# Mixer of a Griffin/attention trunk: four units in the first loop, other places for the first recurrences and the last gates, an output projection in two sums, and modulation rows one per tick

## The chip, the cores and the metric

The kernel runs on one core of a Trainium2 chip. The metric is the device time of one execution in microseconds (us).

## The reference

Two layers on a stream of 1024 frames of width 1024, all in float32. Layer 0 (the mixer, where the change is) is:

```
hn = rms_norm(x) * (1 + scale) + shift          # shift, scale: rows of c_act @ ada_w
gate, xr = split(hn @ w_in)                     # 2 x 1408 columns, 11 tiles of 128 each
xr = causal_depthwise_conv(xr, width 4)
r, i = sigmoid(blocks(xr) @ w_a), sigmoid(blocks(xr) @ w_x)     # 16 blocks of 88 columns
a = exp(-8 * r * softplus(-lam));  u = sqrt(1 - a*a) * (i * xr)
y = scan(y = a * y + u)                         # along the frames
h = x + g1 * ((y * gelu(gate)) @ w_out)
h = h + g2 * (relu(modulated_norm(h) @ w1)**2 @ w2)             # the MLP
```

Layer 1 is chunked attention with an MLP of the same form.

## The kernel before

Every matmul is three (`mm3`, lines L324 to L326): operands are split into a high part (ScalarE, L191) and a low part (VectorE, L195 for weights and for y, L907 for the conv's result, L601 and L792 for normed activations). Activations lie transposed, 128 columns by 1024 frames, so one unit (`proj2`: one tile of 128 columns, both halves of 512 frames) is 48 matmuls.

A class `Stream` lists all that is loaded in order: weights (kind "w"), operands y (kind "a"), modulation rows (kind "u", summed on VectorE at L357) and pre-sums of quadrants (kind "p", L123). It loads through a ring of seven buffers on SyncE's queue, and in each `tick` of the program emits the splits, rows and pre-sums that are due, in list order and as far as a cap per kind lets them. `some(n)` and `gate_item` put rows and the blocks' gate weights into the list; `ws.at(d, ...)` puts work d ticks later. So the order on each engine is what the program writes, tick by tick, and each engine takes its own in that order.

The mixer begins with a loop over the eight tiles of the normed input, in which the norm's work is done tile by tile and the matmuls of the first three units (xr(0), xr(1), gate(0)) accumulate in PSUM at the same time. Then come single units: `xr(t)` makes a tile of xr (ScalarE L879 and L881 take it out of PSUM, VectorE L886 is the conv), copies issued by GpSimd (L894) re-lay the conv's result into blocks of 88 columns, which are split (L900 on ScalarE, L907 on VectorE); `recur(blocks)` does the blocks' gates (sigmoids L933, the product i*x L938, tanh L945, roots and exp L950 and L953) and the scan (L957 to L961); `gate(t)` does a tile of the gate with gelu (L873), and L974 multiplies it with the scan's result, which is stored and loaded again as y. At the end w_out is applied in three sums c = 0, 1, 2 over 3, 4 and 4 tiles of y, each with all eight chunks of 128 output columns; each chunk goes into h at L1059 (`into_h`). Next to the last of them begins the second norm (sq L520, mod L583, statistics L528 to L538), and then the MLP, whose first product w1 is formed by seven products of quadrants (L1209 and L1129 add them).

PSUM has eight banks of 512 columns; a new bank waits until the one that it replaces has been read.

Of the kernel before, what the change touches and what calls it, by code (L numbers as in the profile page):

```python
# [16 lines left out]
KD = 8  # L17
# [48 lines left out]
class Stream:  # L66
# [8 lines left out]
    def __init__(self, nc, slot, wh, ws):  # L75
# [8 lines left out]
        self.hold = None  # L84
        self.timed = self.early = False
# [74 lines left out]
    def ready(self, it, kind, most):  # L160
# [138 lines left out]
def trunk(ctx: ExitStack, tc: tile.TileContext, I, out, dbg=None, stop=None):  # L299
# [102 lines left out]
    w_in(NT, NT + 1, 0, NT + 2, 1)  # L402
    gate_item(_done(0) + _done(1))
    for t in range(3, NT):
        w_in(NT + t)
        some(2 if t < 7 else 0)
        gate_item(_done(t - 1))
        if t < NT - 1:
            w_in(t - 1)
    w_in(NT - 2)  # L410
    gate_item(_done(NT - 1))
    w_in(NT - 1)
    ygd = dp.tile([NT, 128, S], F32, name="ygd")
    ygits = []
    for c in range(3):
        kn = 4 if c else 3
        for _ in range(kn):
# [3 lines left out]
        for j in range(4):  # L421
            ws.add(I["w_out"][c * 4 + j][:, : kn * 256], kn * 256)
            some((2, 2, 0)[c])
# [78 lines left out]
    class Norm:  # L502
# [20 lines left out]
        def mm(self, half):  # L523

            ps = bank()
# [16 lines left out]
        def bc(self, half):  # L542
            ps = bank()
# [195 lines left out]
    for k in range(3, KD):  # L739
# [55 lines left out]
    n1.mm(0)  # L795
    ws.pump(2)
    n1.bc(0)
# [15 lines left out]
    def unit():  # L813
        first.append(ws.next())
        pss.append([bank(), bank()])

    def products(us, half, k):
        c = slice(k * 128, (k + 1) * 128)
        for u in us:
            it = first[u]  # L820
# [4 lines left out]
    unit()  # L825
    unit()
# [3 lines left out]
    n1.mm(1)  # L830
    products((0, 1), 0, 1)
    ada_k(2)
    n1.bc(1)
    moded(2, 0)
    lows(2, 0)
    unit()
# [7 lines left out]
    ada_k(3)  # L844
    for k in range(3):
        lows(k, 1)
        products((0, 1, 2), 1, k)
    for k in range(3, KD):
        moded(k, 0)
        lows(k, 0)  # L850
        normed(1, k)
        if k < KD - 1:
            ada_k(k + 1)
        moded(k, 1)
        lows(k, 1)
        products((0, 1, 2), 0, k)
        products((0, 1, 2), 1, k)
        if k == 6:
            ws.pump(4)
# [95 lines left out]
    def scan(b):  # L955
# [3 lines left out]
        V.tensor_scalar(out=r, in0=r, scalar1=-1.0, scalar2=1.0, op0=ALU.mult, op1=ALU.add)  # L959
        V.tensor_tensor(out=v, in0=v, in1=x, op=ALU.mult)  # L960
# [50 lines left out]
    for half in range(2):  # L1011
        xr_out(0, half, pss[0][half])
    for half in range(2):
        xr_out(1, half, pss[1][half])
    conved(0)
    gelu(0, pss[2])
    for it in first:
        at(1, ws.done, it)
    at(2, conved, 1)
    ws.pump()  # L1020
    xr(2)
    gate(1)
    recur(_done(0) + _done(1))
    for t in range(3, NT):
        xr(t)
        recur(_done(t - 1))
        if t < NT - 1:
            gate(t - 1)
    gate(NT - 2)
# [8 lines left out]
    ws.cap["a"] = 6  # L1038
    gate(NT - 1)
# [4 lines left out]
    k0 = 0  # L1044
    for c in range(3):
        kn = 4 if c else 3
        ys = ygits[k0 : k0 + kn]
        k0 += kn
        its = [ws.next() for _ in range(4)]
        ws.cap["a"] = (14, 16, 8)[c]  # L1050

        def chunk(j, half, e):

            m, it, ps = 2 * j + e, its[j], bank()
            for k in range(kn):
                s = slice(k * 256 + e * 128, k * 256 + e * 128 + 128)
                gh, gl = ys[k]["op"][half]
                mm3(ps, it["hi"][:, s], it["lo"][:, s], gh, gl, k == 0, k == kn - 1)
            V.scalar_tensor_tensor(out=h[m][:, hs(half)], in0=ps, scalar=g1[:, m : m + 1],  # L1059
                                   in1=h[m][:, hs(half)], op0=ALU.mult, op1=ALU.add)  # L1060
            if c == 2:
                final = (half, m) == (1, KD - 1)
                at(int(m < KD - 1), n2.sq, m, hs(half), int(m < KD - 2))

        if c < 2:
            for j in range(4):
                for half in range(2):
                    for e in range(2):
                        chunk(j, half, e)
                        if c == 0 and (j, half, e) in ((0, 0, 1), (0, 1, 1)):  # L1070
                            load_h(2)
                        tick()
                at(1, ws.done, its[j])
        else:

            for j in range(4):
                for e in range(2):
                    chunk(j, 0, e)
                    tick()
            for j in range(4):  # L1080
                for e in range(2):
                    chunk(j, 1, e)
                    n = 2 * j + e
                    if n == 1:
                        n2.mm(0)
                    elif n == 3:
                        n2.bc(0)
                    elif n > 3:
                        n2.mod(0, (n - 4,))
                    ws.tick()  # L1090
                ws.done(its[j])
        ws.live["a"] -= 2 * kn
# [669 lines left out]
```

## Time and profile before

| | |
|---|---|
| median of 3 runs | 2388.7 us (2388.6, 2395.36, 2388.7) |
| profiled execution | 2395.81 us, its span 2394.0 us |
| TensorE busy | 2287.7 us (96%) |
| VectorE busy | 1763.6 us (74%) |
| ScalarE busy | 1246.2 us (52%) |
| TensorE's mean granted clock | 0.985 |
| DMA, mean over the span | 152 GB/s |

A busy share is a mean over all stages; 1.00 of the clock is the full one of 2.4 GHz, 0.50 the lower of its two levels. The mixer's matmuls end at about 490 us of the span.

### The profile page before, as it was taken

What the parts mean: (1) busy time and instruction counts of PE and PEld (TensorE: products, weight loads), DVE (VectorE), ACT (ScalarE), POOL (GpSimd) and SP (SyncE); (2) the same over time, 40 slices, a digit from 0 to 9 for tenths busy, and PEclk for the clock granted to TensorE, in tenths of its full rate; (3) what the DMA queues carried; (4) which work ended last, traced back from release to release, by engine and by line L of the source; (5) the groups of instructions that cost most, each with busy time, mean ns of one, the idle gap of its engine ahead of it and who ended that gap; (6) DMA issues with size and microseconds to landing.
All of it is one profiled execution on the core that took longest, in us unless ns stands there. A gap on an engine that the chain in (4) does not pass through costs nothing.

```text
span 2394.0 us, 31739 instructions
## 1 busy us (share of the span) xinstructions
PE 2287.7 (96%) x11740; PEld 1935.6 (81%) x11740; DVE 1763.6 (74%) x2596; ACT 1246.2 (52%) x2052; POOL 398.7 (17%) x419
## 2 busy tenths in 40 slices
PE   4999989999999899999999999999999999899999
PEld 3778767878877777888999998998888888778887
DVE  8797779588777777778765648997386666778775
ACT  5677873265544643334443229997165555634342
POOL 0001000000000023331000038875000000033322
PEclk9999989999999999999999999999999999999999
DMA  8343349326666774546244200013214444865443
GB/s 306 101 133 106 104 120 314 109 69 220 245 227 236 267 268 147 161 146 228 88 145 131 96 10 10 10 37 122 95 45 165 169 158 163 285 238 161 155 149 133
DMA packets 141640, 363.46 MB, mean 152 GB/s; under 512 B 14924, under 2 KB 17100, under 8 KB 141484
## 3 DMA queue, kind: packets, MB, share of 16 engines
q1 hardware_dynamic: 113756, 278.45, 35.3%
q10 hardware_dynamic: 23824, 71.44, 7.8%
q0 software_dynamic: 3904, 11.54, 1.9%
q8 instruction: 92, 1.51, 0.3%
q14 instruction: 64, 0.52, 0.1%
HBM read 260.19 MB, written 89.65 MB: 146 GB/s over the span
## 4 chain that ended last, share of the span: by engine, by line
PE 65%; DVE 13%; DMA 9%; ACT 8%; issue 4%; POOL 1%; SPq 0%; ACTq 0%; DVEq 0%; POOLq 0%
PE b L325 20%; PE b L326 20%; PE b L324 20%; DMA ws<-in_w_dram 3%; DVE wl L195 2%; DMA hid<-s 2%; PE b L1568 1%; DVE s L195 1%; ACT s L1538 1%; DVE s L357 1%; DMA ws<-hid 1%; ACT s L329 1%; DVE s L1129 1%; POOL ws L123 1%; PE b L1587 1%
## 5 line engine op out<-in xcount | busy, mean ns | idle before, releaser
L324 PE MATMUL b<-s,wh 128*128 128x512 f32 (+1 forms) x2532 | 1004.2, 397 | 43.3 <-DVE s L1231 11.7
L325 PE MATMUL b<-s,wh 128*128 128x512 f32 (+1 forms) x2532 | 998.7, 394 | 19.4 <-DVE s L907 6.5
L326 PE MATMUL b<-s,wl 128*128 128x512 f32 (+1 forms) x2296 | 905.4, 394 | 4.1 <-DVE wl L195 4.1
L324 PEld LDWEIGHTS b<-s,wh 128*128 128x128 f32 (+1 forms) x2532 | 480.0, 190 | 165.0 <-DVE s L1209 13.9
L325 PEld LDWEIGHTS b<-s,wh 128*128 128x128 f32 (+1 forms) x2532 | 479.8, 189 | 128.1 <-DVE s L907 7.4
L191 ACT ACTIVATE wh<-ws 128x1024 fp32r<-128x1024 f32 (+2 forms) x302 | 291.1, 973 | 441.6 <-POOL ws L123 261.1
L326 PEld LDWEIGHTS b<-s,wl 128*128 128x128 f32 (+1 forms) x2296 | 435.1, 190 | 100.1 <-DVE wl L195 5.8
L195 DVE TENSOR_TENSOR wl<-ws,wh 128x1024 fp32r<-128x1024 f32 (+2 forms) x249 | 305.8, 1231 | 113.8 <-ACT wh L191 111.5
L1231 DVE SCALAR_TENSOR_TENSOR s<-b,mod,s 128x512 f32<-128x512 f32 x221 | 165.0, 747 | 88.3 <-PE b L326 88.0
L195 DVE TENSOR_TENSOR s<-ws,s 128x512 fp32r<-128x512 f32 x284 | 223.4, 805 | 0.3 <-ACT s L191 0.3
L123 POOL TENSOR_TENSOR ws<-ws 128x512 f32<-128x512 f32 x21 | 28.4, 1354 | 1165.2 <-DMA s<-hsp 922.3
L324 PE MATMUL b<-wh,s 128*128 128x256 f32 x768 | 216.4, 284 | 0.0
L325 PE MATMUL b<-wl,s 128*128 128x256 f32 x768 | 216.0, 283 | 0.0
L326 PE MATMUL b<-wh,s 128*128 128x256 f32 x768 | 215.2, 283 | 0.5 <-DVE s L562 0.4
L191 ACT ACTIVATE s<-ws 128x512 fp32r<-128x512 f32 x284 | 165.1, 619 | 73.4 <-DMA ws<-ygd 23.7
L325 PEld LDWEIGHTS b<-wl,s 128*128 128x128 f32 x768 | 147.1, 192 | 0.3 <-issue 0.2
L324 PEld LDWEIGHTS b<-wh,s 128*128 128x128 f32 x768 | 147.1, 192 | 0.3 <-issue 0.2
L326 PEld LDWEIGHTS b<-wh,s 128*128 128x128 f32 x768 | 146.5, 192 | 1.0 <-DVE s L562 0.9
L357 DVE CUSTOM_DVE_ANT_0 ws<-ws,cb,vec 128x1024 f32<-128x1024 f32 x59 | 75.3, 1282 | 76.1 <-DMA ws<-in_ada_dram 73.3
L1209 DVE TENSOR_TENSOR s<-s,b 128x512 f32<-128x512 f32 x84 | 57.5, 685 | 99.9 <-PE b L326 88.1
L1207 ACT ACTIVATE s<-b 128x512 f32<-128x512 f32 x84 | 50.0, 596 | 93.2 <-PE b L326 93.0
L1338 ACT ACTIVATE s<-b 128x256 f32<-128x256 f32 x96 | 31.6, 388 | 121.5 <-PE b L326 110.3
(165 smaller groups left out, 3083.7 us busy)
## 6 DMA issues: line engine op xcount, KB each, us to landing
hid<-s ACTq DMA_DIRECT2D x128, 512.0 KB, 5.3
ws<-hid SPq DMA_DIRECT2D x118, 512.0 KB, 4.5
ws<-in_w_dram SPq DMA_DIRECT2D x220, 256.0 KB, 3.4
ws<-in_ada_dram SPq DMA_DIRECT2D x56, 512.0 KB, 3.5
s<-in_ada_dram SPq DMA_DIRECT2D x40, 512.0 KB, 8.8
ws<-in_w_in_dram SPq DMA_DIRECT2D x22, 512.0 KB, 4.6
hsp<-s SPq DMA_DIRECT2D x32, 256.0 KB, 2.0
s<-hsp SPq DMA_DIRECT2D x16, 512.0 KB, 6.9
```

Of the source, the lines that this page charges most:

```text
L123: eng.tensor_tensor(out=out, in0=in0, in1=in1, op=op)
L191: self.nc.scalar.activation(out=hi[:rows, :n], in_=src, func=AF.Copy)
L195: self.nc.vector.tensor_tensor(out=lo[:rows, :n], in0=src, in1=hi[:rows, :n].bitcast(F32), op=ALU.subtract)
L324: PE.matmul(ps, ah, bh, start=start, stop=False, skip_group_check=more)
L325: PE.matmul(ps, ah, bl, start=False, stop=False, skip_group_check=more)
L326: return PE.matmul(ps, al, bh, start=False, stop=stop, skip_group_check=more).ins
L329: A_.activation(out=hi, in_=src, func=AF.Copy)
L357: V.tensor_tensor_reduce(out=t, in0=t, in1=cb, op0=ALU.mult, op1=ALU.add, scale=1.0, scalar=bias, accum_out=dst)
L1207: A_.activation(out=t, in_=ps, func=AF.Copy)
L1209: V.tensor_tensor(out=t, in0=t, in1=ps, op=ALU.add)
L1231: V.scalar_tensor_tensor(out=t, in0=ps, scalar=g2[:, m : m + 1], in1=t, op0=ALU.mult, op1=ALU.add)
L1338: A_.activation(out=d, in_=ps[:, :, e * 128 : (e + 1) * 128], func=AF.Copy)
```

## The change

The first loop holds four units, xr(0), xr(1), gate(0) and xr(2), with the statistics' PSUM banks taken ahead of it; in its last tile the units' matmuls come unit by unit. Behind it come gate(1), xr(3), recur of the blocks of tiles 0 and 1, gate(2), recur of tile 2's, xr(4) and so on. The scan is cut in two, the second part a tick later. At the end gate(10) comes ahead of the last recur, and up to fourteen y operands may be split ahead of it. The output projection takes the first seven tiles of y in one sum, chunk pair by chunk pair, in four PSUM banks, and the last four in a second. Modulation rows come at most one a tick, and their places in the list change. At the start of the MLP the low halves that are due are emitted ahead of the norm's head, and pre-sums are held back until tile 5.

```
         if it["use"]:
-            return True
+            return not self.timed or kind == "p" or self.used < self.now
...
             it["use"](it["need"][0]["st"] if it["raw"] is None else it["st"])
+            self.used = self.now
...
-                if q and self.ready(q[0], kind, most):
+                if q and kind not in self.stop and self.ready(q[0], kind, most):
...
-    w_in(NT, NT + 1, 0, NT + 2, 1)
+    w_in(NT, NT + 1, 0, NT + 2, 1, NT + 3)
     gate_item(_done(0) + _done(1))
-    for t in range(3, NT):
+    w_in(2)
+    gate_item(_done(2))
+    for t in range(4, NT):
         w_in(NT + t)
-        some(2 if t < 7 else 0)
+        some({4: 3, 6: 3, 8: 2}.get(t, 0))
         gate_item(_done(t - 1))
...
+    for j in range(4):
+        if j == 0:
+            yg_items(3)
+        w_out(0, j)
+        if j == 0:
+            yg_items(4)
+        w_out(1, j)
+        some(4)
...
+    norm_banks = [bank() for _ in range(4)]
...
+    ws.pump(4)
     for k in range(3):
         lows(k, 1)
         products((0, 1, 2), 1, k)
+    for half in range(2):
+        for k in range(3):
+            products((3,), half, k)
     for k in range(3, KD):
...
+            for u in range(4):
+                products((u,), 0, k)
+                products((u,), 1, k)
...
         V.tensor_scalar(out=r, in0=r, scalar1=-1.0, scalar2=1.0, op0=ALU.mult, op1=ALU.add)
+        at(1, scan2, b, r, x, tau, v)
+
+    def scan2(b, r, x, tau, v):
         V.tensor_tensor(out=v, in0=v, in1=x, op=ALU.mult)
...
+    for t, u in ((0, 0), (1, 1), (2, 3)):
+        for half in range(2):
+            xr_out(t, half, pss[u][half])
+        if t == 0:
+            conved(0)
+            gelu(0, pss[2])
...
     at(2, conved, 1)
+    at(5, conved, 2)
     ws.pump()
-    xr(2)
     gate(1)
+    xr(3)
     recur(_done(0) + _done(1))
-    for t in range(3, NT):
+    gate(2)
+    recur(_done(2))
+    for t in range(4, NT):
         xr(t)
         recur(_done(t - 1))
-        if t < NT - 1:
-            gate(t - 1)
-    gate(NT - 2)
+        gate(t - 1)
+    ws.cap["a"] = 14
+    gate(NT - 1)
     recur(_done(NT - 1))
...
-    ws.cap["a"] = 6
-    gate(NT - 1)
     load_h(4)
...
+    chunks = [(half, e) for half in range(2) for e in range(2)]
+    for j in range(4):
+        if j == 2:
+            ws.cap["a"] = 22
+        its = [ws.next() for _ in range(2)]
+        pss = [bank() for _ in chunks]
+        for c, ys in enumerate((ygits[:3], ygits[3:7])):
+            for ps, (half, e) in zip(pss, chunks):
+                part_of(ps, its[c], e, half, ys, c == 0, c == 1)
+                if c:
+                    into_h(2 * j + e, half, ps)
+                elif j == 0 and half == 0:
+                    load_h(2)
+                tick()
+            at(1, ws.done, its[c])
...
+            ws.flush()
             head(k, nrm, l == 0)
+            ws.stop = ("p",) if k < 5 else ()
```

Three places of the order that this makes. The first is VectorE just before the gates of blocks 5 and 6, whose low halves are L907 (L940 in the changed file). Before, the last recurrence ahead of them was followed by one weight's low half:

```order
202 L938 TENSOR_TENSOR s_931<-s_1106,s_931 88x1024
203 L957 SCALAR_TENSOR_TENSOR s_1133<-s_1105,s_1133 88x1024
204 L958 SCALAR_TENSOR_TENSOR s_1105<-s_1105,s_1131 88x1024
205 L959 TENSOR_SCALAR s_1105<-s_1105 88x1024
206 L960 TENSOR_TENSOR s_1133<-s_1133,s_931 88x1024
207 L961 SCALAR_TENSOR_TENSOR s_1131<-s_1105,s_1133 88x1024
208 L195 TENSOR_TENSOR wl_1220<-ws_849,wh_1219 128x1024
209 L907 TENSOR_TENSOR s_1242<-s_1149,s_1215 88x1024
210 L907 TENSOR_TENSOR s_1244<-s_1152,s_1217 88x1024
```

In the changed program:

```order
192 L997 SCALAR_TENSOR_TENSOR s_998<-s_966,s_1002 88x1024
193 L1010 TENSOR_TENSOR s_704<-s_704,s_1045 128x1024
194 L990 SCALAR_TENSOR_TENSOR s_1116<-s_1085,s_1116 88x1024
195 L991 SCALAR_TENSOR_TENSOR s_1085<-s_1085,s_1114 88x1024
196 L992 TENSOR_SCALAR s_1085<-s_1085 88x1024
197 L996 TENSOR_TENSOR s_1116<-s_1116,s_856 88x1024
198 L997 SCALAR_TENSOR_TENSOR s_1114<-s_1085,s_1116 88x1024
199 L200 TENSOR_TENSOR wl_1212<-ws_777,wh_1211 128x1024
200 L940 TENSOR_TENSOR s_1233<-s_1135,s_1207 88x1024
201 L940 TENSOR_TENSOR s_1235<-s_1138,s_1209 88x1024
```

So the same five recurrences and five conv stand ahead of these lows in both, from conv(0) on (row 131 before, row 127 now), while conv(0) itself now comes behind a first loop with one unit more.

The second is TensorE behind gate(9), whose last bank is b_2321 before and b_2315 now. Before, the last blocks' gates (88 rows) come next:

```order
1178 L324 MATMUL b_2321<-s_510,wh_2093 128x512
1179 L325 MATMUL b_2321<-s_511,wh_2093 128x512
1180 L326 MATMUL b_2321<-s_510,wl_2094 128x512
1181 L324 MATMUL b_2366<-s_2334,wh_1889 88x512
1182 L325 MATMUL b_2366<-s_2352,wh_1889 88x512
```

Now gate(10) (b_2354) comes next:

```order
1178 L329 MATMUL b_2315<-s_555,wh_2093 128x512
1179 L330 MATMUL b_2315<-s_556,wh_2093 128x512
1180 L331 MATMUL b_2315<-s_555,wl_2094 128x512
1181 L329 MATMUL b_2354<-s_243,wh_2186 128x512
1182 L330 MATMUL b_2354<-s_244,wh_2186 128x512
```

The 48 matmuls of gate(10) have moved ahead of the 24 of the last gates, which begin at row 1229 now.

The third is VectorE in the MLP's w1 loop, one of its rounds. Before, pre-sums (L123) and three modulation rows (L357, each with the reading of its sum) stand ahead of the last add (L1209):

```order
601 L1209 TENSOR_TENSOR s_4137<-s_4137,b_4141 128x512
602 L123 TENSOR_TENSOR ws_4085<-ws_4175 128x512
603 L123 TENSOR_TENSOR ws_4135<-ws_4175,ws_4085 128x512
604 L123 TENSOR_TENSOR ws_4132<-ws_4135,ws_4175 128x512
605 L123 TENSOR_TENSOR ws_4132<-ws_4135,ws_4132 128x512
606 L357 ISA s_4178,mod_83<-s_4178,cb,vec 128x1024
607 L357 ISA mod_83 128x1
608 L357 ISA s_4180,mod_83<-s_4180,cb,vec 128x1024
609 L357 ISA mod_83 128x1
610 L357 ISA s_4182,mod_83<-s_4182,cb,vec 128x1024
611 L357 ISA mod_83 128x1
612 L1209 TENSOR_TENSOR s_4138<-s_4138,b_4139 128x512
```

Now (pre-sums L126, rows L362, adds L1256 and L1174):

```order
601 L1256 TENSOR_TENSOR s_4250<-s_4250,b_4254 128x512
602 L126 TENSOR_TENSOR ws_4200<-ws_4290 128x512
603 L126 TENSOR_TENSOR ws_4248<-ws_4290,ws_4200 128x512
604 L126 TENSOR_TENSOR ws_4245<-ws_4248,ws_4290 128x512
605 L126 TENSOR_TENSOR ws_4245<-ws_4248,ws_4245 128x512
606 L1256 TENSOR_TENSOR s_4251<-s_4251,b_4252 128x512
607 L1174 TENSOR_TENSOR s_4104<-s_4103,s_4104 128x512
608 L1174 TENSOR_TENSOR s_4103<-s_4103 128x512
609 L1174 TENSOR_TENSOR s_4103<-s_4103,s_4104 128x512
610 L1174 TENSOR_TENSOR s_4104<-s_4104,s_4103 128x512
611 L362 ISA s_4293,mod_83<-s_4293,cb,vec 128x1024
612 L362 ISA mod_83 128x1
```

The add comes right behind the pre-sums, and the rows follow later, one at a time between other instructions.

## Rows read from the trace of the kernel before

**Rows 1.** The page: busy time, share of the span and instructions of two engines.

```profile
PE 2287.7 (96%) x11740; PEld 1935.6 (81%) x11740; DVE 1763.6 (74%) x2596; ACT 1246.2 (52%) x2052; POOL 398.7 (17%) x419
```

**Rows 2.** TensorE's waits between 100 and 520 us: total us, times, longest.

```profile
PE b L325 <- DVE s L907: 6.5, 2, 5.9
PE b L324 <- ACT s L900: 6.3, 1, 6.3
PE b L325 <- DVE s L601: 5.9, 2, 3.5
PE b L325 <- DVE s L195: 3.3, 3, 2.8
PE b L324 <- ACT s L873: 2.5, 1, 2.5
```

**Rows 3.** TensorE's waits between 580 and 770 us.

```profile
PE b L324 <- DVE s L1209: 6.5, 8, 1.6
```

**Rows 4.** TensorE by stretch: length, busy (matmuls), clock, DMA share, GB/s.

```profile
60.00:91.73 31.73, 31.73 (x141) 1.00 0.16 41
109.41:116.41 7.00, 7.00 (x18) 0.55 0.00 1
158.41:168.41 10.00, 10.00 (x27) 0.57 0.46 135
338.00:353.00 15.00, 14.47 (x37) 0.56 0.35 100
```

**Rows 5.** All engines by stretch: PE, PEld, DVE, ACT, POOL, clock, DMA share.

```profile
186.76:318.00 131.24, 131.24 (x578) 105.02 (x577) 100.80 (x84) 105.80 (x125) 11.99 (x23) 1.00 0.33 96
375.10:443.00 67.90, 67.90 (x301) 56.22 (x300) 58.53 (x81) 15.32 (x21) 0.53 (x1) 1.00 0.74 255
```

**Rows 6.** VectorE's groups by form, 124 to 186 us: busy us, mean ns.

```profile
L195 DVE TENSOR_TENSOR wl<-ws,wh 128x1024 fp32r<-128x1024 f32 x4 | 4.9, 1218 | 0.3 <-ACT wh L191 0.3
L357 DVE CUSTOM_DVE_ANT_0 ws<-ws,cb,vec 128x1024 f32<-128x1024 f32 x3 | 3.8, 1268 | 0.0
L195 DVE TENSOR_TENSOR wl<-ws,wh 88x704 fp32r<-88x704 f32 x1 | 0.9, 882 | 0.0
```

**Rows 7.** VectorE's timeline, conv(0) and (1), and lows of blocks 5, 6.

```profile
80.99 7.75 DVE L886 SCALAR_TENSOR_TENSOR s<-s,vec,s 128x1023 f32<-128x1023 f32 x6 [3.44 <-ACT s L881]
...
181.31 2.35 DVE L907 TENSOR_TENSOR s<-s,s 88x1024 fp32r<-88x1024 f32 x2
```

**Rows 8.** VectorE's timeline, 322 to 388 us: start, length, instruction.

```profile
325.65 1.22 DVE L974 TENSOR_TENSOR s<-s,s 128x1024 f32<-128x1024 f32 x1
326.79 3.91 DVE L886 SCALAR_TENSOR_TENSOR s<-s,vec,s 128x1023 f32<-128x1023 f32 x3
...
341.62 1.22 DVE L957 SCALAR_TENSOR_TENSOR s<-s,s 88x1024 f32<-88x1024 f32 x1
...
348.19 0.93 DVE L195 TENSOR_TENSOR wl<-ws,wh 128x768 fp32r<-128x768 f32 x1
...
373.18 0.74 DVE L1059 SCALAR_TENSOR_TENSOR s<-b,mod,s 128x512 f32<-128x512 f32 x1
```

**Rows 9.** ScalarE's timeline, 318 to 376 us.

```profile
336.86 1.06 ACT L900 ACTIVATE s<-s 88x1024 fp32r<-88x1024 f32 x1 [7.18 <-DMA s<-s]
...
359.60 3.22 ACT L191 ACTIVATE s<-ws 128x512 fp32r<-128x512 f32 x6
```

**Rows 10.** TensorE by stretch, 370 to 388 us: busy, clock, DMA share, GB/s.

```profile
370.00:388.00 18.00, 17.09 (x68) 0.91 1.03 360
```

**Rows 11.** VectorE's timeline behind the MLP's first statistics.

```profile
501.58 1.22 DVE L195 TENSOR_TENSOR wl<-ws,wh 128x1024 fp32r<-128x1024 f32 x1
...
503.32 2.13 DVE L123 TENSOR_TENSOR ws<-ws,ws 128x512 f32<-128x512 f32 x3
```

**Rows 12.** VectorE's timeline in the w1 loop, one round.

```profile
679.94 1.28 DVE L357 CUSTOM_DVE_ANT_0 s<-s,cb,vec 128x1024 f32<-128x1024 f32 x1
...
683.56 0.68 DVE L1209 TENSOR_TENSOR s<-s,b 128x512 f32<-128x512 f32 x1
```

More of the change, by code (lines that the diff above doesn't have):

```diff
@@ L420, in trunk, with w_out @@
                                  dep=k))
-        for j in range(4):
-            ws.add(I["w_out"][c * 4 + j][:, : kn * 256], kn * 256)
-            some((2, 2, 0)[c])
+    def w_out(c, j):
+        kn = 4 if c else 3
+        ws.add(I["w_out"][c * 4 + j][:, : kn * 256], kn * 256)
+    for j in range(4):
[6 more added lines that the diff above has]
+        some(4)
+    yg_items(4)
+    for j in range(4):
+        w_out(2, j)
     rest = rest[:8] + part(1, 1) + part(1, 0)
@@ L540, in mm, with bc @@
             self.dg = dg
-        def bc(self, half):
-            ps = bank()
+        def bc(self, half, ps=None):
+            ps = ps or bank()
             PE.matmul(ps, ones, self.dg[:, :HALF], start=True, stop=True)
@@ L738, in trunk @@
     ws.load(3)
-    for k in range(3, KD):
+    load_ada(3)
+    ws.load(4)
+    for k in range(4, KD):
         load_ada(k)
@@ L811, in trunk @@
     first, pss = [], []
-    def unit():
-        first.append(ws.next())
-        pss.append([bank(), bank()])
+    for u in range(4):
+        first.append(ws.next)
+        pss.append([bank(), None])
     def products(us, half, k):
@@ L819, in products @@
         for u in us:
+            if callable(first[u]):
+                first[u] = first[u]()
+            if pss[u][half] is None:
+                pss[u][half] = bank()
             it = first[u]
@@ L847, in trunk @@
         products((0, 1, 2), 1, k)
+    for half in range(2):
+        for k in range(3):
+            products((3,), half, k)
     for k in range(3, KD):
+        normed(1, k)
         moded(k, 0)
-        lows(k, 0)
-        normed(1, k)
+        moded(k, 1)
         if k < KD - 1:
             ada_k(k + 1)
-        moded(k, 1)
+        lows(k, 0)
         lows(k, 1)
[L856 to L859, printed above, removed]
+        if k < KD - 1:
+            products(range(4), 0, k)
+            products(range(4), 1, k)
+        else:
+            for u in range(4):
+                products((u,), 0, k)
+                products((u,), 1, k)
+                if u == 0:
+                    ws.live["w"] -= first[0]["cost"]
+                    ws.pump(5)
     ws.timed = True
@@ L1043, in trunk @@
     n2 = NormS(h, aa[:, 8:16], mods[0][:, 24:32])
[L1044 to L1092, printed above, removed]
@@ new lines, in part_of, with into_h @@
+    def part_of(ps, it, e, half, ys, first, last):
+        n = len(ys)
+        for k, y in enumerate(ys):
+            s = slice(k * 256 + e * 128, k * 256 + e * 128 + 128)
+            gh, gl = y["op"][half]
+            mm3(ps, it["hi"][:, s], it["lo"][:, s], gh, gl, first and k == 0, last and k == n - 1)
+    def into_h(m, half, ps):
+        V.scalar_tensor_tensor(out=h[m][:, hs(half)], in0=ps, scalar=g1[:, m : m + 1],
+                               in1=h[m][:, hs(half)], op0=ALU.mult, op1=ALU.add)
@@ new lines, in trunk @@
+    chunks = [(half, e) for half in range(2) for e in range(2)]
+    for j in range(4):
+        if j == 2:
[11 more added lines that the diff above has]
+            at(1, ws.done, its[c])
@@ new lines, in trunk, with chunk @@
+    ws.live["a"] -= 14
+    ws.cap["a"] = 8
+    its = [ws.next() for _ in range(4)]
+    def chunk(j, half, e):
+        m, ps = 2 * j + e, bank()
+        part_of(ps, its[j], e, half, ygits[7:], True, True)
+        into_h(m, half, ps)
+        at(int(m < KD - 1), n2.sq, m, hs(half), int(m < KD - 2))
+    for j in range(4):
+        for e in range(2):
+            chunk(j, 0, e)
+            tick()
+    for j in range(4):
+        for e in range(2):
+            chunk(j, 1, e)
+            n = 2 * j + e
+            if n == 1:
+                n2.mm(0)
+            elif n == 3:
+                n2.bc(0)
+            elif n > 3:
+                n2.mod(0, (n - 4,))
+            ws.tick()
+        ws.done(its[j])
```

37 lines of the change are left out of this document (14 added, 23 removed).

## The prediction

> **What bounds the kernel now.** The page's first part is read first: TensorE is busy for 2287.7 us of a span of 2394.0, VectorE for 1763.6 [rows 1]. TensorE sets the time, so a change is worth what it takes from TensorE's idle time and from the stretches in which its clock is low after such idle time. The number of matmuls stays the same, so nothing else can be won there. The second view, TensorE's waits by line, says which waits those are in the mixer and just behind it: between 100 and 520 us five lines cost 24.5 us [rows 2], and in the first MLP eight waits for the add L1209 cost 6.5 us [rows 3]. The third view, busy time by stretch, says what the waits cost beyond themselves. At full clock 141 matmuls take 31.73 us, 0.225 us each; in the ten us behind the wait that ends at 158.41 only 27 run, at a mean clock of 0.57, so 10.0 - 27 x 0.227 = 3.9 us are lost on top; behind the wait of 109.41 it is 7.0 - 18 x 0.227 = 2.9, and in 338 to 353, where 37 run, 15.0 - 8.4 = 6.6, of which 0.5 is idle time [rows 4]. (0.227 is from the long busy stretch: 131.24 us with 578 matmuls and no idle time [rows 5].) From the end of the first loop with its xr(2), 91.73, to the start of the third sum of the output projection, 443.0, the program has 1392 matmuls: 1392 x 0.227 = 316 us of work in 351. So the mixer holds 35 us to be won at most, the MLP's start some 6, and the adds 6.5.
>
> **The change, part by part.** I put the edits where the trace has waits, and walk each queue in the new order with the old durations.
>
> *First loop, four units, and the first recurrences.* The fourth unit's low half is one more L195, 1.22 us, ahead of the low halves that TensorE waits for, with its ScalarE split ahead of it [rows 6]: I take 1.5 us later, between 0 (the engine waits for other lows anyway) and 2.5 (both in a row). The matmuls of xr(2) now run inside the loop, so it ends where xr(2) ended, 91.7 + 1.5 = 93.2. But unit 0 comes out only 3 x 6 matmuls before that, at 89.1, so conv(0), which started at 80.99, starts at about 92.5 [rows 7]: 11.5 us later. From there VectorE's queue up to the low halves of blocks 5 and 6 (L907, L940 after) holds, counted in the new order: five conv of 3.91 us (19.5), five recurrences of 6.57 (341.62 to 348.19: 32.9), seven full splits and two of 704 columns (some 9.6), six ada rows of 1.2 (7.2), seven lows, five products and two gated products of 1.14 each (16.0): 85.2 us [rows 6, 8]. (An instruction starts some 0.07 us before the one ahead of it ends, as L974 and the conv behind it show, so these are times from start to start.) The same count of before, with one split and two rows more, is 88.7, and it took 80.99 to 183.66 [rows 7], so VectorE idled for 14 us in it. Without any idle time the lows would be out at 177.7, with the old idle time at 191.7. My walk leaves 8.5 us of waits (for ScalarE's exp and sigmoids, and for three wh), since the recurrences now start a unit later and the rest of the queue is ready: 185.0 for block 5, 186.2 for block 6. TensorE would be there at 93.2 + 348 x 0.227 = 172.2, plus one short wait of a gelu, 1 us or so: 173.6. The two old waits, 2.5 for a gelu and 5.9 for the lows of block 4, and their 2.9 and 3.9 of low clock fall away [rows 2, 4]; in their place comes one of 11.4 us with 3.9 of low clock. The 24 matmuls of those gates then end at 185.0 + 5.4 + 3.9 + 0.6 (the second low) = 194.9, against 186.76 + 5.5 = 192.3 before [rows 5]. So this part, which takes two waits away, **costs 2.6 us** (177.7 gives -5, 191.7 gives +9).
>
> *The steady part*, tiles 5 to 9: VectorE works 100.80 and ScalarE 105.80 of 131.24 us, and TensorE waits for nothing [rows 5]. The scan in two ticks and the other counts of ada rows lie in this slack, at nothing; were VectorE full there, the five rows that leave and come would be worth 1.2 us each.
>
> *Last gates behind the last unit.* Now the 24 matmuls of the last blocks' gates come right behind gate(9), and wait 6.3 us for the split L900, which waits 7.18 for the copies of conv(10)'s result [rows 2, 9]. With gate(10) in between, 48 x 0.227 = 10.9 us of other work cover the 6.3 and the 0.5; the 6.1 of low clock behind go too. If gate(10) were not there the 6.8 would be back. What is late next: ScalarE has fourteen y splits in front of gelu(10) instead of six behind everything. Six took 3.22 us [rows 9], so fourteen take 7.5, and gelu(10) moves to about 348.5; the third bank of the last block's gates is one of gate(10)'s, and TensorE is there at 346.6. So it waits some 2 us. In the trace of before the six stand between the exps and gelu(10), which starts only when they are done. The Trainium skill (PSUM — Partial Sum Buffer, section Engine vs sequencer instructions) says that ScalarE's and VectorE's queues are strict FIFO; by that a later gelu cannot pass the fourteen splits, and the trace agrees. If it could, the 2 us would be nought.
>
> *Output projection in two sums.* Sixteen into_h (L1059) fewer, some 0.74 us each [rows 8], 12 us of VectorE; TensorE doesn't wait for them now, so this is worth nothing by itself. But the second sum now stands in the first four banks' place, 36 matmuls (8.2 us) behind the first, and needs the weights of c=1, whose low half stands on VectorE behind the y lows, and whose load falls into the burst of loads of h: the 16 engines' share is 1.03, at 360 GB/s, between 370 and 388 [rows 10]. I get that low half at 373.3, and TensorE there at 371: a wait of 2.5 instead of the old 2.8 for L195 [rows 2], and as before some 1.5 of low clock. With 0.9 for the first bank and the low clock behind the 2 us, TensorE comes to the third sum at about 433 (443 before); without any wait, 318.0 + 468 x 0.227 = 424.2. So the end of the mixer **gives 10 us** (2 if the burst holds the weights for 8 us more, 19 if no wait is left).
>
> The Trainium skill (DMA: Bandwidth & Descriptors, section Issuing engines are not separate DMA queues) says that transfers started by different engines run on the same 16 DMA engines and interleave; this speaks against the change, which brings a load into the burst, and the full share agrees.
>
> *The MLP's start.* Two waits for the low halves L601 cost 5.9 there, the longest 3.5 [rows 2]. The four pre-sums L123, 0.7 us each [rows 11], stood between the lows and now come after them; the flush puts the second group of lows ahead of the statistics. I take the second wait, 5.9 - 3.5 = 2.4, with its low clock, 1.5: **gives 4** (2 if the low clock stays, 6 if the first wait shortens too).
>
> *Rows one a tick.* In the w1 loop three rows stand right ahead of an add L1209, which starts 3.6 us after the first of them [rows 12]; eight times TensorE waits for it, 6.5 us in all [rows 3]. Now the add comes ahead of the rows and these lie between splits, so the waits go: **gives 6.5** (4 if single rows still catch an add). None of these leaves a low clock in the row.
>
> **The sum**: 2.6 - 10.4 - 4 - 6.5 = -18.3. The profiled execution took 2395.81 us, 1.8 more than its span and 7.1 more than the median of the three runs, 2388.7. I take the same waits for the median run: 2388.7 - 18.3 = 2370.4, some 2371 (by the profiled execution 2377.5).
>
> **Rivals.**
> 1. *All of it is won.* VectorE has no idle time after conv(0) (lows at 177.7, -5.3 in the first part), the last gates and both sums run without a wait (-19), the MLP's start gives 6: -5.3 - 19 - 6 - 6.5 = -37, 2352. For it: the work is there early enough by the counts. Against it: VectorE had 14 us of waits in the same stretch.
> 2. *The first part pays for the last.* The old 14 us of idle time stay (+9), and the weights of the second sum come late in the burst (-2): +9 - 2 - 4 - 6.5 = -3.5, 2385. For it: the same chain of conv, copies and splits stands in both orders, and the DMA share is full.
> 3. *The MLP half does nothing.* The rows and pre-sums have to be done on VectorE somewhere; the waits move to the next split or add: 2.6 - 10.4 = -8, 2381. Against it: VectorE's slack, 26% of the span [rows 1].
> 4. *Slower.* One mechanism: conv's result reaches the gates by copies that ScalarE's split waits for, 7.18 us at tile 10 [rows 9], and in VectorE's queue a low half that waits holds the next conv. If VectorE waits 7.2 for each of the first five tiles, that is 36 us instead of 8.5, the lows of block 5 come at 212.5, and the sum is -18.3 + 27.5 = +9: 2398. It is slower from about 210 on (18.3 + 7.2 later than 185). Against it: before, the same stretch had 14 us of idle time in all.
>
> **How the numbers follow.** About 0.3%, 7.2 us, is what a measurement of this kernel can tell from no change: faster is under 2381.5, slower over 2395.9. My forecast has 0.55 (its own range 2361 to 2380, from the bounds of the first part and of the end, of which not all fall on one side), rival 1 0.14, rival 2 0.12, rival 3 0.11, half of it on each side of the bound, rival 4 0.08. Faster: 0.55 + 0.14 + 0.06 = 0.75; same: 0.12 + 0.05 = 0.17; slower: 0.08. The range reaches from rival 1, 2352, to just past rival 2, 2386.
>
> **What would show it.** In the profile of the changed kernel: no TensorE wait for the lows of block 4 nor for the gelu in front of the first gates; one wait of 7 to 16 us for L940 near 185, with a low clock behind it; none for L933 at the last gates, one of some 2 us for L906, one of 2 to 3 for L200 at the start of the second sum; the third sum starting near 433 plus what the first part moved; one wait for L619 instead of two; none for L1256. I am wrong if the L940 wait is missing or over 20 us, or if the second sum waits for its weights for over 8 us.

## The result: 2389.8 to 2376.4 us, and the profile after

Median of four runs each: 2389.8 us before, 2376.4 after, a ratio of 0.9936 [0.9916, 0.9957]. Timed again with more runs (run r2 below) it was 2390.0 and 2373.8, 0.9928 [0.9911, 0.9945]. So the change takes off 13 to 16 us; forecast were 18. One of the ten runs of r5 below took 5829 us and is left out of its numbers.

The page of the changed kernel, busy time by engine, beside [rows 1]; then TensorE's waits from 40 to 530 us and from 530 to 780 us (total, times, longest), beside [rows 2, 3], which have 100 to 520 and 580 to 770:

```profile
PE 2276.8 (96%) x11740; PEld 1932.3 (81%) x11740; DVE 1751.4 (74%) x2580; ACT 1242.1 (52%) x2051; POOL 398.9 (17%) x419
```

```profile
PE b L330 <- DVE s L940: 10.4, 1, 10.4
PE b L330 <- DVE s L812: 5.3, 2, 5.0
PE b L330 <- DVE s L619: 3.7, 2, 3.4
PE b L329 <- ACT s L966: 1.5, 2, 0.9
PE b L329 <- ACT wh L196: 1.4, 1, 1.4
PE b L329 <- ACT s L906: 1.1, 1, 1.1
PE b L562 <- DVE s L556: 0.9, 1, 0.9
PE b L331 <- DVE wl L200: 0.8, 1, 0.8
```

```profile
PE b L329 <- DVE s L1256: 4.0, 3, 3.1
```

The reader is to see that most lines of before are gone or smaller: the split, L900 of before with 6.3, does not appear under its new line L933, and the gelu, L906 now, has 1.1 instead of 2.5. The lows, L907 of before and L940 now, are the exception: their waits of 6.5, of which 5.9 stood at block 4, have become one of 10.4 at blocks 5 and 6, the largest of the mixer. L812 stands in the first loop, where before had one wait of 3.5 for the same low halves (L792). Three instructions of VectorE's timeline of the changed kernel say when the 10.4 came about: conv(0), the first part of the first recurrence, which waited 2.31 us for ScalarE's exp, and the lows of blocks 5 and 6.

```profile
91.80 3.92 DVE L919 SCALAR_TENSOR_TENSOR s<-s,vec,s 128x1023 f32<-128x1023 f32 x3 [1.09 <-ACT s L914]
...
132.21 1.22 DVE L990 SCALAR_TENSOR_TENSOR s<-s,s 88x1024 f32<-88x1024 f32 x1 [2.31 <-ACT s L986]
...
183.71 2.35 DVE L940 TENSOR_TENSOR s<-s,s 88x1024 fp32r<-88x1024 f32 x2
```

Both programs have the same number of matmuls, so the traces can be laid side by side, the first matmul beside the first and so on, and each stage's share read off as the change of the difference between their start times (plus means that the changed kernel loses there). In us, the first profiled execution of before against the changed kernel, and beside it a second execution of before (run r1):

```
stage (where it ends)                     forecast   first trace   second trace
front, to behind the gates of blocks 5, 6    +2.6       +3.8          +9.1
end of the mixer, to the third sum          -10.4      -13.6         -13.7
the MLP's start                              -4.0       -4.4          -6.1
w1 of the first MLP                          -6.5       -4.3          -5.9
all behind it                                 0         -1.0          +1.5
to the last matmul                          -18.3      -19.5         -15.1
```

### The profile page after: what moved, and what is told of

Same layout as the page of the kernel before. It is cut to its first block, busy times and chain, and to the rows that moved or that the text cites. A ratio compares the mean times of both kernels' runs of the same rounds, so it can differ in the third digit from the quotient of the medians.

```text
span 2374.5 us, 31723 instructions
## 1 busy us (share of the span) xinstructions
PE 2276.8 (96%) x11740; PEld 1932.3 (81%) x11740; DVE 1751.4 (74%) x2580; ACT 1242.1 (52%) x2051; POOL 398.9 (17%) x419
## 4 chain that ended last, share of the span: by engine, by line
PE 66%; DVE 11%; DMA 10%; ACT 7%; issue 4%; POOL 1%; ACTq 0%; SPq 0%; DVEq 0%; POOLq 0%
PE b L330 20%; PE b L331 20%; PE b L329 20%; DMA hid<-s 5%; DMA ws<-in_w_dram 3%; DVE wl L200 2%; PE b L1615 2%; ACT s L1585 1%; DVE s L200 1%; DVE s L1174 1%; ACT s L334 1%; DMA ws<-hid 1%; POOL ws L126 1%; PE b L1634 1%; PE b L1635 1%
## 5 line engine op out<-in xcount | busy, mean ns | idle before, releaser
L330 PE MATMUL b<-s,wh 128*128 128x512 f32 (+1 forms) x2532 | 995.4, 393 | 19.3 <-DVE s L940 10.4
L126 POOL TENSOR_TENSOR ws<-ws 128x512 f32<-128x512 f32 x21 | 27.7, 1319 | 1144.7 <-DMA s<-hsp 463.8
L196 ACT ACTIVATE s<-ws 128x512 fp32r<-128x512 f32 x284 | 164.0, 618 | 55.0 <-DMA ws<-hid 22.2
L362 DVE CUSTOM_DVE_ANT_0 ws<-ws,cb,vec 128x1024 f32<-128x1024 f32 x59 | 75.2, 1280 | 74.9 <-DMA ws<-in_ada_dram 72.2
L1256 DVE TENSOR_TENSOR s<-s,b 128x512 f32<-128x512 f32 x84 | 57.3, 683 | 73.4 <-PE b L331 66.9
```

Of the source, the lines that this page charges most:

```text
L126: eng.tensor_tensor(out=out, in0=in0, in1=in1, op=op)
L196: self.nc.scalar.activation(out=hi[:rows, :n], in_=src, func=AF.Copy)
L330: PE.matmul(ps, ah, bl, start=False, stop=False, skip_group_check=more)
L362: V.tensor_tensor_reduce(out=t, in0=t, in1=cb, op0=ALU.mult, op1=ALU.add, scale=1.0, scalar=bias, accum_out=dst)
L1256: V.tensor_tensor(out=t, in0=t, in1=ps, op=ALU.add)
```

## The experiments

Twelve runs, in three groups; each group was timed against the kernel before on its own chip. r9 to r12 are of another group than r2 and r4, and the intervals of r11 and r12 overlap that of r4, so between those the traces decide. "Trace" below means a comparison matmul by matmul as above. In the cuts of code, `...` stands for lines left out.

**r1, the kernel before again.** 

> The kernel before, unchanged. Its profiled execution took 2395.81 us and the median of its runs 2388.7, so an execution can be 7 us longer without any change. Theory: those 7 us lie outside the stages that the change touches (they come from transfers, in the attention or the second MLP), so that in a shorter execution the five mixer lines that TensorE waits for (L907, L900, L601, L195, L873) still cost about 24.5 us and the adds L1209 in the first MLP about 6.5. Rival: they lie in those stages, and a shorter execution shows some 17 us for the five lines, or none for the adds; then the gain of the change is smaller by those 7 us in most executions. Ratio 1.000 within 0.002 by both.

Measured: 1.0001 [0.9989, 1.0013], the profiled execution 2391.4 us. The rival holds for the front, though not with its number: behind the first gates this execution is 5.3 us ahead of the first one, and behind those of blocks 5 and 6 still 5.2, but the four lines of the five that it has left cost 22.2 us and not 17. Its waits from 100 to 520 us:

```profile
PE b L325 <- DVE s L907: 6.6, 2, 6.1
PE b L324 <- ACT s L900: 6.4, 1, 6.4
PE b L325 <- DVE s L601: 5.6, 2, 3.4
PE b L325 <- DVE s L195: 3.6, 4, 2.8
PE b L324 <- ACT s L933: 1.4, 2, 1.1
```

The wait of 2.5 for gelu, L873, is not among them. ScalarE's timeline says why: first the execution of before that the prediction used, then this one. The split of tile 2's blocks (tiles count from 0) waits for the copies of the conv's result in both, but these land 4.1 us earlier in the second. Of that, 1.2 are from the first loop, which was ahead by as much (GpSimd issued the copies at 97.50 instead of 98.71), and 2.9 are the copies themselves.

```profile
105.90 1.06 ACT L900 ACTIVATE s<-s 88x1024 fp32r<-88x1024 f32 x1 [9.87 <-DMA s<-s]
```

```profile
101.84 1.06 ACT L900 ACTIVATE s<-s 88x1024 fp32r<-88x1024 f32 x1 [7.02 <-DMA s<-s]
```

The gelu stands behind that split on ScalarE. So of the 5.2 us some 4 are the late copies, with the wait for the gelu and the low clock behind it, less the 1.1 that TensorE waits for sigmoids (L933) in the second execution alone; what put the first loop 1.2 behind is open. Of the nine traces of kernels with the old front, two (the first of before, and r5) show a wait of 2.4 us or more there, seven 0.9 or less.

**r2, the changed kernel again.** 

> The changed kernel, unchanged. Profiled, it was 19.5 us shorter than the profiled execution of before, but 13.4 us by the medians. Theory: the parts are worth +3.8 at the front, -13.6 at the end of the mixer, -4.4 at the MLP's start and -4 to -5 for the rows, some -18, and the ratio is 0.992 to 0.993. Rival: 7 us of that were only in the one profiled execution of before, and the ratio is 0.9945 or so, -13.

Measured: 0.9928 [0.9911, 0.9945], 2373.8 us. The ratio is the theory's; by the medians it is -16.1, between the two numbers. The trace of the front fits that: the late copies count in some executions only.

**r3, lows of tile 4 two ticks earlier.**

```
-        at(5 if late else 3, split_hi, t)
-        at(6 if late else 4, split_lo, t)
+        at(4 if t == 4 else 5 if late else 3, split_hi, t)
+        at(4 if t == 4 else 6 if late else 4, split_lo, t)
```

> The changed kernel, with the split of tile 4's blocks (5 and 6) asked for two ticks earlier, so that their two low halves stand on VectorE ahead of block 4's recurrence and a weight's low half instead of behind them: 7.7 us earlier. Theory: the 10.4 us wait is the place of two instructions in VectorE's queue, nothing more. TensorE is there at 174.6, the first low comes at 177.2 instead of 184.9: a wait of 2.6, and 7.7 us less in all, up to 11 if the low clock behind the wait goes as well; 0.990 to 0.9905 of before, and no new wait in the next 40 us. Rival: VectorE is the bound up to there, and a low half that is taken out of turn makes block 4's recurrence late; the wait comes back within the next two units, at a product or at the next lows, and the time is that of the changed kernel.

Measured: 0.9907 [0.9891, 0.9923], 2367.8 us, 6.0 below the changed kernel, a little under the theory's 7.7. Its first line of waits between 100 and 360 us:

```profile
PE b L330 <- DVE s L940: 2.7, 1, 2.7
```

The wait is 2.7, as the theory said. By the trace the gain is 7.9 us behind the gates, 9.2 at the end of the first MLP's w1 and 6.5 at the last matmul, so it does not come back as another wait. So the wait was a matter of the place of two low halves (their high halves on ScalarE moved with them).

**r4, the old front under the changed rest.** Its edit is the diff of the front (the list, the first loop, the order of units) taken back; the order of units, of it:

```
+    xr(2)
     gate(1)
-    xr(3)
     recur(_done(0) + _done(1))
-    gate(2)
-    recur(_done(2))
-    for t in range(4, NT):
+    for t in range(3, NT):
```

> The changed kernel with the front of before: three units in the first loop, then xr(2), gate(1), the recurrences of tiles 0 and 1, xr(3) and so on, and rows two for each of four tiles in that part of the list; the last gates, the two sums, the rows and the MLP's start as changed. Theory: four units cost 3.8 us net, so this is 3 to 4 us below the changed kernel, with the two old waits (2.5 for a gelu, 5.9 for block 4's lows) back in place of the one of 10.4, and the end of the mixer as changed; 0.991 to 0.992. Rival: with the old front, rows one a tick and the scan in two ticks make block 4's lows later than before, the old 5.9 grows, and nothing is won against the changed kernel.

Measured: 0.9881 [0.9863, 0.9899], 2362.2 us: 11.6 below the changed kernel, three times the theory's 3 to 4. The old waits come back smaller than they were: 2.9 for block 4's lows where before had 5.9, and none of 2.5 for a gelu. So against this front the four units cost some 12 us; the trace has 12.0 behind the gates of blocks 5 and 6.

**r5, rows one a tick from the first MLP on.**

```
         if it["use"]:
-            return True
+            return not (self.timed and self.single) or kind == "p" or self.used < self.now
...
+            self.used = self.now
...
+    ws.single = True
```

> The kernel before with one edit: from the first MLP on, at most one modulation row a tick. Theory: the waits for the add L1209 in the first MLP go, 6.5 us in the first profile of before and 7.3 in the second, and 4 to 5 us of that stay won; 0.998 of before. Rival: the rows have to be done on VectorE somewhere, so the waits move to the low halves or to the adds of w2, and the time is that of before. Either is near what the runs can tell; the two traces, matmul by matmul, decide it.

Measured: 0.9969 [0.9952, 0.9986], -5.9 us by the medians. No wait for the add L1209 is left before 730 us; three are left in the last rounds, 3.7 us with the longest 1.8. Against r1's trace, counted from the end of the mixer, it wins 6.8 us up to the end of w1, and 4.6 of them are left at the end of the first MLP. The theory holds, with its size.

**r6, the MLP's start alone.**

```
-                if q and self.ready(q[0], kind, most):
+                if q and kind not in self.stop and self.ready(q[0], kind, most):
...
+            ws.flush()
             head(k, nrm, l == 0)
+            ws.stop = ("p",) if k < 5 else ()
```

> The kernel before with the MLP's start as changed: the due low halves ahead of the norm's head, and pre-sums held back until tile 5. Theory: the second wait for the lows L601 there, 2.2 to 2.5 us, and the low clock behind it, 1.5, go: 3.5 to 4.4 us at the next tiles, 0.998 to 0.9985 of before. Rival: the pre-sums that are held back make a weight of the fourth or fifth tile late, and 2 us or more are given back within 40 us.

Measured: 0.9996 [0.9982, 1.0010], no difference that the times can tell (the medians lie 4.1 us apart). Against r1's trace it is 2.8 us ahead behind the MLP's first tiles, and 1.3 to 3.6 through the first product. TensorE's waits for the lows L602 there are 3.7, the longest 3.5, instead of 5.6: the second one is gone, the first stays.

**r7, gate(10) ahead of the last gates, three sums kept.**

```
-        if t < NT - 1:
-            gate(t - 1)
-    gate(NT - 2)
+        gate(t - 1)
+    ws.cap["a"] = 6
+    gate(NT - 1)
     recur(_done(NT - 1))
...
-    ws.cap["a"] = 6
-    gate(NT - 1)
```

> The kernel before with gate(10) ahead of the last blocks' gates, six y splits as before ahead of gate(10)'s end, the output projection in three sums. Theory: this edit is what the end of the mixer gains: the wait of 6.3 for L900, the 0.5 behind it and their low clock of some 6 go, 10 to 13 us by the start of the second sum, with the wait of 2.8 for L195 still there; 0.995 of before. Rival: without the two sums the y splits and gelu(10) stand in the way: a wait of 4 us or more for the gates' banks or for the first y, and at most 6 us are left; 0.9975.

Measured: 0.9985 [0.9972, 0.9997], -4.8 us by the medians. In the trace some 13 us are won up to three quarters of the first sum, and 10 are given back in the next 25 us. Its waits between 340 and 480 us show to what:

```profile
PE b L324 <- DVE s L1055: 7.7, 3, 4.6
PE b L325 <- DVE s L195: 1.5, 1, 1.5
PE b L324 <- ACT s L931: 0.9, 1, 0.9
```

L1055 is into_h. With gate(10) moved, TensorE reaches the first sum's chunks while VectorE still has the last recurrences, and three times a bank waits for an into_h that stands behind one. Neither theory named that wait.

**r8, two sums, gate(10) where it was.** Its edit is the diff's new output projection and its list, on the kernel before. 

> The kernel before with the output projection in two sums and the weights' and y's places in the list that go with it, up to fourteen y splits, and gate(10) where it was, behind the last gates. Theory: TensorE doesn't wait for the sixteen into_h that go, so nothing is won by them, and the second sum's weights in the burst of loads cost as much as L195 did: within 2 us of before, 0.999 to 1.001. Rival: with gate(10) last, fourteen y splits stand right behind it and the first sum can't start until the y of tiles 3 to 6 are split: 3 to 8 us slower, 1.002 to 1.003.

Measured: 1.0017 [1.0003, 1.0031], 2395.2 us, 3.9 above before by the medians. The theory falls; it is the rival's size, by another wait than it named. Of TensorE's waits between 320 and 480 us the longest and the one for the split, which is L912 here:

```profile
PE b L326 <- DVE wl L195: 12.5, 1, 12.5
PE b L324 <- ACT s L912: 1.7, 1, 1.7
```

The long wait in TensorE's timeline; then the high half of those weights on ScalarE; then VectorE, with the start of the last recurrence and the low half that TensorE waits for:

```profile
374.16 0.80 PE L326 MATMUL b<-s,wl 128*128 128x512 f32 x1 [12.54 <-DVE wl L195]
```

```profile
359.24 1.06 ACT L191 ACTIVATE wh<-ws 128x1024 fp32r<-128x1024 f32 x1
```

```profile
362.80 1.22 DVE L969 SCALAR_TENSOR_TENSOR s<-s,s 88x1024 f32<-88x1024 f32 x1
...
372.89 1.21 DVE L195 TENSOR_TENSOR wl<-ws,wh 128x1024 fp32r<-128x1024 f32 x1
```

These are the first weights of the second sum. They had landed and their high half was out at 360.3, so it is not the burst of loads that holds them: their low half stands on VectorE behind the last recurrence, the low halves of y and a gated product. Up to that wait r8 is 9.6 us ahead of before, counted from the end of its own front, although gate(10) stands where it was: the split waits 2.63 us for its copies instead of 7.18, and TensorE 1.7 for it instead of 6.3.

**r9, units of the first loop earlier.**

```
-        if k < KD - 1:
+        if k < 5:
             products(range(4), 0, k)
             products(range(4), 1, k)
-        else:
+        elif k == KD - 1:
             for u in range(4):
-                products((u,), 0, k)
-                products((u,), 1, k)
+                for x in range(5, KD):
+                    products((u,), 0, x)
+                    products((u,), 1, x)
```

> The changed kernel with one edit on TensorE alone: in the first loop the matmuls of the last three tiles, not only of the last, come unit by unit, so that unit 0 is out 36 matmuls, 8.2 us, earlier (81 instead of 89) and the loop ends when it did. VectorE's and ScalarE's orders stay word for word. Theory: the changed front is late because conv(0) is; VectorE is full from there to the lows of block 5, so these move with conv(0): conv(0) at some 83.6, the lows at 177 instead of 185, the wait 2 to 3 us instead of 10.4, and 8 to 11 us less than the changed kernel; 0.989 of before. Rival: what holds the lows is not conv(0) but the waits in between (ScalarE's exps and sigmoids, which come when TensorE brings the gates); VectorE gets its idle time back there, and 3 us or less are won.

Measured: 0.9936 [0.9919, 0.9953], 2375.4 us: nothing. The theory falls. Busy time by stretch (PE, PEld, DVE, ACT, POOL, clock, DMA share), first of the changed kernel, then of this one, each from conv(0) to the first recurrence and from there to the lows of blocks 5 and 6:

```profile
91.80:132.21 40.41, 40.41 (x179) 32.30 (x178) 33.25 (x34) 32.37 (x43) 4.43 (x8) 1.00 0.57 170
132.21:183.71 51.50, 40.46 (x176) 31.40 (x174) 48.78 (x41) 42.72 (x50) 5.51 (x11) 0.94 0.35 106
```

```profile
83.04:131.62 48.58, 48.58 (x215) 39.06 (x214) 33.36 (x34) 32.75 (x43) 4.43 (x8) 1.00 0.49 142
131.62:183.11 51.49, 42.07 (x176) 32.57 (x174) 48.76 (x41) 42.71 (x50) 5.48 (x11) 0.93 0.34 106
```

conv(0) started at 83.0 instead of 91.8, and VectorE simply idled for 15 us instead of 7 before the first recurrence, which starts at 131.6 instead of 132.2. From there VectorE is busy for 48.8 of 51.5 us in both. So what holds the lows is the first recurrence and not conv(0). That it waits for ScalarE's exps, and these for gates that TensorE has only after gate(1) and xr(3), is read from the changed kernel's trace (first gates at 114.3, sigmoids from 117.0, the exps at 131.0), and no run has moved the gates.

**r10, four units, lows and the fourth split moved.** r9 with r3's edit, and `ws.pump(4)` behind the third tile's lows. 

> The kernel of the run before with two more edits: tile 4's splits asked for two ticks earlier, and the fourth unit's split behind the third tile's lows in the first loop instead of ahead of all three. Theory: the waits add up as separate ones: 10.4 and its 3.9 of low clock go whole, and the 1.5 of the first loop, 14 to 16 us below the changed kernel and below the old front too: 2358 to 2361, 0.9865 to 0.988. Rival: with TensorE at the gates of block 5 by 172 it meets the copies of conv(4) instead, and a wait of 4 us or more stands there; then it is no better than the old front, 0.988.

Measured: 0.9902 [0.9880, 0.9924], 2364.8 us. The waits went as forecast (1.0 is left at the gates of block 5, and the trace is 18 us ahead of r2's at the second sum), but only 12 us of it are left at the last matmul; the rest goes in stages that no edit touches. The ratio misses the theory's, and why is open. The time is no better than the old front's, as the rival said, but its wait of 4 us or more is not there.

**r11, the old front with lows of tiles 3 and 4 one tick earlier.**

```
-        at(6 if late else 4, split_lo, t)
+        at(5 if t in (3, 4) else 6 if late else 4, split_lo, t)
```

> The old front under the changed rest, with the lows of tile 3 (block 4) and tile 4 (blocks 5 and 6) asked for one tick earlier. Theory: the wait of 2.9 at 151 is the place of one low half behind a gated product and a row; it goes, with up to 3 us of low clock, and the lows of blocks 5 and 6 now come at 173.6, when TensorE wants them at 172: 4 to 6 us below the old front, 0.986. Rival: VectorE is the bound up to block 6, so the wait moves to those gates or to the units behind them, and the time is that of the old front, 0.988.

Measured: 0.9861 [0.9842, 0.9880], 2357.5 us, 4.7 below r4, and the best of all; by the trace it is 5.0 ahead of r4 at the end of the front. Its waits from 100 to 360 us:

```profile
PE b L329 <- ACT s L949: 1.9, 3, 1.0
PE b L329 <- ACT wh L196: 1.4, 1, 1.4
PE b L330 <- DVE s L923: 0.9, 1, 0.9
PE b L331 <- DVE wl L200: 0.7, 1, 0.7
```

**r12, the old front with the scan in one piece.**

```
-        at(1, scan2, b, r, x, tau, v)
-
-    def scan2(b, r, x, tau, v):
```

> The old front under the changed rest, with the scan in one piece as before. In the order this puts each recurrence's product and scan, 3.4 us, ahead of the lows of block 4 and ahead of the lows of the last blocks again. Theory: with the old front, block 4's lows came 3 us earlier than before because the scan is cut in two; with it whole the wait goes from 2.9 back to some 6, with a longer low clock: 3 to 5 us above the run with the old front, 0.990. Rival: the 3 us come from the rows, one a tick; then the wait stays 2.9 and the time at 0.988.

Measured: 0.9902 [0.9883, 0.9920], 2368.7 us, 6.5 above r4 by the medians. Its first line of waits from 100 to 360 us:

```profile
PE b L330 <- DVE s L923: 6.1, 1, 6.1
```

The theory holds: from the first recurrence to block 4's lows it is 32.5 us here and 29.3 in r4, so the cut in the scan lets them in 3.2 us earlier, and by the trace that is its worth at the end of the front, 3.2 us.

## Why the prediction was right or wrong

*The whole.* 2371 was forecast, 2376.4 and 2373.8 measured; the direction and the range held. Against the profiled execution that the terms were read from, the sum was off by 1.2 us (-19.5 for -18.3), and that is in part luck: the parts, in the order of the table, were off by +1.2, -3.2, -0.4, +2.2 and -1.0, which cancel. The step that failed for the median is "I take the same waits for the median run": the 2.5 us wait for a gelu and its 2.9 of low clock were late copies of that one execution (r1), so taking them away is worth some 4 us against it and nothing against most others.

*The front.* Its times came as worked out: the first loop's wait 1.6 us longer (1.5 forecast), conv(0) at 91.8 (92.5), the lows wanted from 174.6 (173.6), out at 185.0 (185.0), a wait of 10.4 (11.4). Mis-sized was the low clock behind the wait, put at 3.9 as behind the old wait of 5.9. In the changed kernel 24 matmuls run in 185 to 195 and 58 in 185 to 204, so 19.0 - 58 x 0.227 = 5.8 us are lost:

```profile
185.00:195.00 10.00, 10.00 (x24) 0.50 0.67 209
185.00:204.00 19.00, 19.00 (x58) 0.67 0.50 153
```

So +3.8 against the first trace, +9.1 against the second, and 12 against an old front with the cut scan (r4): the scan, costed at nothing, is worth 3.2 there (r12) and hides that much of what the four units cost. And the reason was wrong though the number fitted, which is luck too: I counted VectorE's queue from conv(0), and 85.2 us of work with 8.5 of waits gave 185. r9 shows that a conv(0) 8.8 us earlier moves the lows by 0.6. The chain starts at the first recurrence, 132.2, and that is late because the change puts the first gates behind a unit more (114.3 instead of 102.6). A slip without weight: by the steps that gave 2.6, the two bounds of this part are -5.9 and +8.1 and not -5.3 and +9.

*The end of the mixer*, -13.6 for -10.4. TensorE no longer waits for the split, as forecast, but gate(10) is only part of the reason. In the changed kernel the split waits 2.58 us for its copies instead of 7.18 [rows 9], and r8, with gate(10) in its old place, has 2.63; first the changed kernel, then r8:

```profile
336.11 1.06 ACT L933 ACTIVATE s<-s 88x1024 fp32r<-88x1024 f32 x1 [2.58 <-DMA s<-s]
```

```profile
328.43 1.06 ACT L912 ACTIVATE s<-s 88x1024 fp32r<-88x1024 f32 x1 [2.63 <-DMA s<-s]
```

TensorE has done gate(9) at 335.4 and the split is out at 337.2, so what gate(10) covers here is some 2 us by an estimate from these two times, where I had 6.3; with the old list it covers the whole (r7). What makes the copies earlier was not tested on its own. Before, two modulation rows stood on VectorE shortly ahead of conv(10) (at 316.7 and 324.5) and loads of further rows were asked for around the copies (at 327.3 and 334.4); in r8 and in the changed kernel neither is there.

Then ScalarE takes fourteen y splits, 7.39 us, ahead of gelu(10), as two rows of the changed kernel's timeline of ScalarE show:

```profile
342.31 7.39 ACT L196 ACTIVATE s<-ws 128x512 fp32r<-128x512 f32 x14
349.60 1.06 ACT L906 ACTIVATE s<-b 128x512 f32<-128x512 f32 x2
```

The 2 us that I gave this were 0.7, for the sigmoids behind it. The weights' wait of 2.5 was 1.4 + 0.8, near the time that I named but at another place: at the second chunk pair's weights, whose split waited for their load, and not at the second sum, whose low half was out in time. First that low half, then that split:

```profile
360.01 1.21 DVE L200 TENSOR_TENSOR wl<-ws,wh 128x1024 fp32r<-128x1024 f32 x1
```

```profile
372.56 0.84 ACT L196 ACTIVATE wh<-ws 128x768 fp32r<-128x768 f32 x1 [6.03 <-DMA ws<-in_w_out_dram]
```

What failed is to take the moved gate and the two sums one by one, the sixteen into_h as "worth nothing by itself". That is so without the moved gate: alone the two sums cost 4 us (r8). But alone the moved gate keeps only 4 of its 13 (r7), and together they gain 13.6. In both runs TensorE ends up waiting for something that stands on VectorE behind the last recurrences, an into_h in r7 and the weights' low half in r8. In the changed kernel the last recurrences start at 365.5, behind that low half, and no into_h is wanted during the first 36 matmuls. This reading is from the traces; no run divides the 13.6 further.

*The MLP's start*, -4.4 for -4.0: of the two waits for L619 one of 3.4 is left, beside one of 0.2. Alone it is 1.3 to 3.6 (r6). *The rows*, -4.3 to -5.9 for -6.5, and -6.8 alone in that stage (r5). Of the adds' waits 4.0 us stay, 3.1 of them in one. There VectorE's pre-sums waited 5.06 us for a load, so a transfer holds it first; but a single row of 1.2 us stands right ahead of the add that TensorE waits for, as the bound of 4 had it:

```profile
758.77 0.69 DVE L126 TENSOR_TENSOR ws<-ws 128x512 f32<-128x512 f32 x1 [5.06 <-DMA ws<-in_w_dram]
...
763.77 1.28 DVE L362 CUSTOM_DVE_ANT_0 s<-s,cb,vec 128x1024 f32<-128x1024 f32 x1
...
764.97 0.68 DVE L1256 TENSOR_TENSOR s<-s,b 128x512 f32<-128x512 f32 x1
```

*The rivals.* None of the four came true as a whole. The fourth, slower by late copies, named the thing that moved the result: copies were late, but in the kernel before.

Open stay why r10 gives back 5 to 7 us behind the mixer, what four units would do with the first gates a unit earlier, which was not tried, and how much of the end's 13.6 us is the list and how much gate(10).

## What to carry to other kernels

Where two engines are nearly full, ask which chain a wait hangs on before moving its first link: r9 moved the conv by 8.8 us for nothing, while r3 and r11 moved two or three instructions in a queue and won 5 to 6 us each. Test the parts of a change apart: here one part cost 12 us that the others paid for, and two parts that are worth 4 us and less than nothing alone are worth 13.6 together. And look at a second execution before adding a trace's waits to a median: one wait of 2.5 us with its low clock was there in two of nine.

## What the runs showed of the hardware

The same copies issued by GpSimd took 2.9 us longer in one execution of a program than in another (ScalarE waited 9.87 and 7.02 us for them), while VectorE's and ScalarE's own instructions repeat to some hundredths (the first two conv took 7.75 us in both). After a wait of 10.4 us TensorE's clock stayed at 0.50, 1.2 GHz, for all of the next 10 us, where behind waits of 2.5 and 5.9 it was 0.55 and 0.57 over 7 and 10 us [rows 4].
